# Recurrent branch of a hybrid decoder layer: v's rows turned a step later, scan first in the next step, a norm's end behind the splits, sample sums a step later

## The chip, the cores and the metric

The kernel runs on one core of one Trainium2 chip. The metric is the device time of one execution in microseconds (us), as the median of several runs; a profiled execution stands beside it. Engines are named as the profile does: PE (TensorE matmul), PEld (its weight load), DVE (VectorE), ACT (ScalarE), POOL (GpSimd), SP (SyncE, which issues most DMAs).

## The reference, cut to what matters

One decoder layer is computed for 512 prompt tokens and 8 sample tokens together (520 columns): a dilated window attention and a recurrent branch side by side, a gated merge, and a mixture of experts. The recurrent branch has 8 heads with keys and values of 128:

```
q_hg = silu(qh);  f = lb + (1 - lb) * sigmoid(fh);  k_hg = 1 - f;  logf = log(f)
b = cumsum(logf)                                     # per chunk
attn[t,s] = sum_k q[t] k[s] exp(b[t] - b[s])         # s <= t
o = (q * exp(b)) @ state + attn @ v
new_state = exp(b_last) * state + (k * exp(b_last - b))^T v
hg = rms_norm(o, hg_norm_w) * silu(gh)               # per head
y = sigmoid(ga) * (att @ w_br_a) + sigmoid(gb) * (hg @ w_br_b)
```

The samples take one step each from their own cached state (`hgrn_s`); the attention's sample tokens read the three caches.

## The kernel before, in words

Everything lies transposed: channels on partitions, 520 columns along the free axis. Every product of the layer is made from two-part weights: a raw block of 128x1024 is loaded, ACT makes the high part (`whi`, L132), DVE the rest (`wlo`, L133), and PE runs 24 pairs of matmuls of 260 columns (`proj`, L180). `weights_in` keeps the loads four and the splits three blocks ahead, issuing them at the start of the step.

In the recurrent stage the order of every engine's queue is the order in which the program issues instructions. A head has five steps, each with one product: f, q, v, gg (the gate gh) and one block of the merge's gates (`gate`). Ahead of each product, `step_all` runs `beside`: first the DMAs left over by `after` in the step before, then the next piece of each running generator. The generators are `chain(h)`, one per head; each lives for ten steps, so two of them run at any time. `decode_attention` is a further generator, advanced once per step and twice in every fourth (SP loads cache rows, POOL multiplies, DVE sums).

The pieces of `chain(h)`, by the step in which they run: (q) logarithm on ACT, scan on DVE; (v) kd, exponentials, decays of levels 0 and 1; (gg) v's rows: one small transpose for the samples (`pts`, L783) and four for the prompt (`ptm`, L788), copied by ACT to `vs` and `vt`, then q times k (L800), sides 0 and 1, decays 2; (gate) k's rows `kt`, pair matmuls of levels 0 and 1 (L758, L761), decays 3, and the load of the sample states `ss`; (next f) pairs 2, decays 4 and 5; (q) pairs 3, sides 4 and 5, ACT scales `ss`; (v) pairs 4 and 5, `neighbours` (L746), and the sample sums, eight additions of v times k to `ss` on DVE (L836); (gg) pairs 6, the states (L846 on PE, L853 on DVE); (gate) the outputs `po` and `pos`, copied by ACT to `ob`, and its square; (f after that) `finish`: the norm's matmul (L383), the root on ACT (L384), reciprocal (L385), weighting (L386) and gate (L876) on DVE. `decays(i)` are two DVE subtractions (L733, L734) and an exponential on ACT (L735); `sides(i)` are two DVE products (L739, L740).

The matmuls of the chain write to four rotating banks (`bank`), the products to two double ones (`pair_bank`). The program outside this stage (from the splits of `att` and `hg` on) is ordered by the framework's own planner.

Of the kernel before, what the change touches and what calls it, by code (L numbers as in the profile page):

```python
# [11 lines left out]
F32 = mybir.dt.float32  # L12
# [5 lines left out]
AF = mybir.ActivationFunctionType  # L18
ALU = mybir.AluOpType
# [4 lines left out]
P = 128  # L24
D = 1024
KC = D // P
NT = 512
NS = 8
# [57 lines left out]
def layer(ctx, tc, A, O, K):  # L86
    nc = tc.nc
    act, dve, pool, pe, dma, dma2 = nc.scalar, nc.vector, nc.gpsimd, nc.tensor, nc.sync, nc.sync
# [4 lines left out]
    ident = cp.tile([P, P], F32, name="ident")  # L93
# [22 lines left out]
    d_hv = dr.tile([8, NS, P], F32, name="d_hv")  # L116
# [11 lines left out]
    def split(hi, lo, src, eng=None, first=None):  # L128
        if first:
            first.tensor_copy(hi, src)  # L130
        else:
            act.activation(hi, src, AF.Copy)  # L132
        return (eng or dve).tensor_tensor(out=lo, in0=src, in1=hi.bitcast(F32), op=ALU.subtract)  # L133
# [12 lines left out]
    def bank(name="pa"):  # L146
        return banks[-1].tile([P, 512], F32, tag="pa", name=name)
# [25 lines left out]
    def proj(src, kc, xhi, xlo, eng=None, w=None):  # L173
        whi, wlo = w or wload(src, kc, P, eng)
        ps = pair_bank()
        for k in range(kc):
            first, last = k == 0, k == kc - 1
            for w, x, n in ((whi, xhi, 0), (whi, xlo, 1), (wlo, xhi, 2)):
                for s in range(2):
                    pe.matmul(ps[:, s, :NH], w[:, k, :], x[:, k, s * NH:(s + 1) * NH],  # L180
                              start=first and n == 0, stop=last and n == 2)
        return ps
# [57 lines left out]
    hT_hi = fp.tile([P, KC, N], F32R, name="hT_hi")  # L240
    hT_lo = fp.tile([P, KC, N], F32R, name="hT_lo")


    with tc.tile_pool(name="st", bufs=1) as st:
# [9 lines left out]
        rs = st.tile([P, N], F32, name="rs")  # L254
# [31 lines left out]
    att = xp.tile([P, 4, N], F32, name="att")  # L286
# [53 lines left out]
    def weights_in():  # L340

        k = at_[2]
        at_[2] += 1
        while at_[0] < min(len(plan), k + 4):
            src, kc = plan[at_[0]]
            parts[at_[0]] = wtile("raw", F32, RAW)
            dma.dma_start(parts[at_[0]].rearrange("p (k c) -> p k c", k=kc), src)
            at_[0] += 1
        while at_[1] < min(len(plan), k + 3):
            hi, lo = wtile("whi", F32R, 3), wtile("wlo", F32R, 3)  # L350
            split(hi, lo, parts[at_[1]])
            parts[at_[1]] = [x.rearrange("p (k c) -> p k c", k=plan[at_[1]][1]) for x in (hi, lo)]
            at_[1] += 1
        return parts.pop(k)

    def product():
        return proj(None, KC, hT_hi, hT_lo, None, weights_in())

    late = []

    def after(f):

        late.append(f)

    def begin():
        todo, late[:] = late[:], []
        for f in todo:
            f()

    def norm_bc(x, lhsT, w, pl):  # L370

        sq = pl("sq", F32)
        act.activation(sq, x, AF.Square)
        parts = [sq]
        if lhsT.dtype == F32R:
            parts = pl("shi", F32R), pl("slo", F32R)
            split(*parts, sq, pool)

        def finish():
            ps, rs = pair_bank(), pl("rs", F32)  # L380
            for s in range(2):
                for i, t in enumerate(parts):
                    pe.matmul(ps[:, s, :NH], lhsT, t[:, s * NH:(s + 1) * NH], start=i == 0, stop=i == len(parts) - 1)  # L383
            act.activation(two(rs), half(ps), AF.Sqrt, bias=eps)  # L384
            dve.reciprocal(rs, rs)  # L385
            dve.scalar_tensor_tensor(out=x, in0=x, scalar=w, in1=rs, op0=ALU.mult, op1=ALU.mult)  # L386

        return finish

# [64 lines left out]
    with tc.tile_pool(name="at", bufs=2) as at:  # L454
# [9 lines left out]
        xs_, vtm, norms_ = {}, {}, {}  # L464
# [97 lines left out]
        def second_norms(hp):  # L562

            yield
            yield
            for n in range(6):
                norms_.pop((hp, n))()
                yield

        def qkv(hp, n):  # L570
# [116 lines left out]
    hg = mix.enter_context(tc.tile_pool(name="hgo", bufs=1, side="right")).tile([P, KC, N], F32, name="hg")  # L687
    with tc.tile_pool(name="da", bufs=2) as da, tc.tile_pool(name="hgp", bufs=2) as hp_:
# [10 lines left out]
        def t2(name):  # L699
            return hp_.tile([P, N], F32, tag="t2", name=name, bufs=T2)[:, :NT]  # L700

        w = hp_.tile([P, 9 * 64], F32, name="w", bufs=1)
# [6 lines left out]
        def chain(h):  # L709
            d = heads[h]  # L710
            f, k = d["f"], d["k"]
            lf = t2("lf")
            act.activation(lf, f[:, :NT], AF.Ln)
            bb = t2("bb")
            dve.tensor_tensor_scan(bb, reset, lf, 0.0, op0=ALU.mult, op1=ALU.add)
            yield
            q = d["q"]
            kd, eb = t2("kd"), t2("eb")
            bl = t128(bb)[:, :, P - 1:P]
# [59 lines left out]
            yield  # L779

            v = d["v"]
            pts = bank("pts")
            pe.transpose(out=pts[:NS, :P], in_=v[:, NT:], identity=ident)  # L783

            def rows(src, name):
                pt = bank("ptm")
                for i in range(4):
                    pe.transpose(out=pt[:, i * P:(i + 1) * P], in_=src[:, i * P:(i + 1) * P], identity=ident)  # L788
                dst = t2(name)
                act.activation(dst, pt, AF.Copy)  # L790
                return dst

            vs = hp_.tile([NS, P], F32, tag="vs", name="vs")
            act.activation(vs, pts[:NS, :P], AF.Copy)
            after(lambda: dma2.dma_start(d_hv[h], vs))
            vt = rows(v, "vt")
            pl = bank("pl")
            for a in range(4):
                c = slice(a * P, (a + 1) * P)
# [6 lines left out]
            sides(1)  # L806
            dve.tensor_mul(qb, q[:, :NT], eb)
            yield
            kt = rows(kd, "kt")
            placed = [pairs(0), pairs(1)]  # L810
            sides(2)
            decays(3)
            for x in placed:
                x()
            ss = hp_.tile([P, NS, P], F32, tag="ss", name="ss", bufs=2)
            dma2.dma_start(ss, A["state_hgrn"][h])
            vb = hp_.tile([P, NS, P], F32, tag="vb", name="vb", bufs=1)
            after(lambda: dma2.dma_start(vb, d_hv[h:h + 1].to_broadcast([P, NS, P])))
            yield
            placed = [pairs(2)]  # L820
            sides(3)
            decays(4)
# [9 lines left out]
            yield  # L832
            placed = [pairs(4), pairs(5)]
            neighbours()
            for b in range(NS):
                dve.scalar_tensor_tensor(out=ss[:, b], in0=vb[:, b], scalar=k[:, NT + b:NT + b + 1], in1=ss[:, b],  # L836
                                         op0=ALU.mult, op1=ALU.add)
            for x in placed:
                x()
            after(lambda: dma2.dma_start(O["hgrn_s"][h], ss))  # L840
            yield
            placed = pairs(6)
            pk = bank("pkv")
            for a in range(4):
                c = slice(a * P, (a + 1) * P)
# [3 lines left out]
            for a in range(4):  # L849
                c = slice(a * P, (a + 1) * P)  # L850
                new = hp_.tile([P, P], F32, tag="state", name="state", bufs=4)
                if a:
                    dve.scalar_tensor_tensor(out=new, in0=states[-1], scalar=eb[:, (a + 1) * P - 1:(a + 1) * P], in1=pk[:, c],  # L853
                                             op0=ALU.mult, op1=ALU.add)
                else:
                    dve.tensor_copy(new, pk[:, c])
                states.append(new)
            after(lambda: dma2.dma_start(O["hgrn_p"][h], states[3]))
            yield
            po = bank("po")  # L860
            for a in range(4):
                c = slice(a * P, (a + 1) * P)
# [7 lines left out]
            ob = hp_.tile([P, N], F32, tag="t2", name="ob", bufs=T2)  # L870
            act.activation(ob[:, :NT], po, AF.Copy, scale=0.5)
            act.activation(ob[:, NT:], pos[:, :NS], AF.Copy, scale=0.5)
            finish = norm_bc(ob, ones_v, half_w, lambda n, dt: hp_.tile([P, N], dt, tag="t2", name=n, bufs=T2))
            yield
            finish()
            dve.tensor_mul(hg[:, h], ob, d["gg"])  # L876

        decode = decode_attention(da)
        late_steps = [0]

        def step_all():
            beside()
            late_steps[0] += 1
            for _ in range(2 if late_steps[0] % 4 == 0 else 1):
                next(decode, None)


# [8 lines left out]
                    flows.append(chain(h + 1))  # L896
        while flows:
            step_all()
        begin()
        for _ in decode:  # L900
            pass
# [7 lines left out]
    a_hi = xp2.tile([P, 4, N], F32R, name="a_hi")  # L909
    a_lo = xp2.tile([P, 4, N], F32R, name="a_lo")  # L910
# [2 lines left out]
    y_hi = yp.tile([P, KC, N], F32R, name="y_hi")  # L913
    y_lo = yp.tile([P, KC, N], F32R, name="y_lo")
    for c in range(4):
        split(a_hi[:, c], a_lo[:, c], att[:, c], pool if c % 2 else dve)
    for c in range(KC):
        split(g_hi[:, c], g_lo[:, c], hg[:, c], pool if c % 2 else dve)
    for c in range(KC):
# [40 lines left out]
    for c in range(KC):  # L960
# [3 lines left out]
        if c == 0:  # L964
            with tc.issue_after(last.ins):
# [4 lines left out]
                                 op0=ALU.mult, op1=ALU.add)  # L970
# [11 lines left out]
    rs = yblk("rs")  # L982
# [334 lines left out]
    for k, _ in enumerate(choose_tile(3, sel3)):  # L1317
        if k % 3 == 0:
            ahead(pool)
    dve.scalar_tensor_tensor(out=idx3, in0=sel3[:, 1].rearrange("p h k -> p (h k)"), scalar=128.0,  # L1320
                             in1=sel3[:, 2].rearrange("p h k -> p (h k)"), op0=ALU.mult, op1=ALU.add)
# [91 lines left out]
    cs, vr, vs, gts = {}, {}, {}, {}  # L1413
# [61 lines left out]
    rows = [(k < P) + (20 <= k < 148) + (148 <= k < 156) + (160 <= k) for k in range(n_sparse)]  # L1475
# [44 lines left out]
    x = x_rows(d_x[3], P)  # L1520
# [71 lines left out]
```

## Time and profile before

| what | value |
|---|---|
| median of 3 runs | 2453.06 us (2452.21 to 2458.89) |
| profiled execution | 2453.66 us |
| its span | 2451.9 us |
| mean granted TensorE clock | 0.962 |
| PE busy | 2297.9 us (94%) |
| PEld busy | 2118.4 us (86%) |
| DVE busy | 1760.3 us (72%) |
| ACT busy | 1155.0 us (47%) |
| POOL busy | 660.6 us (27%) |

The span is the time from the first to the last instruction; the profiled execution's own time lies 1.8 us above it. Busy shares are means over the whole kernel, whose stages have different limits. A granted clock of 1.00 is 2.4 GHz, 0.50 is 1.2 GHz, and a value between is a mean over a stretch that held both.

### The profile page before, as it was taken

The page shows a single profiled execution, that of the slowest core. Times are in us where ns is not written, and L with a number is a line of the kernel's source. Part 1 is how long each engine was busy: PE and PEld are TensorE (multiplying, and loading weights), DVE is VectorE, ACT ScalarE, POOL GpSimd, SP SyncE. Part 2 cuts the span into 40 slices and gives each one's busy share as a digit, 9 for nine tenths or more (in the row PEclk, how much of TensorE's full clock was granted, in tenths as well). Part 3 has the DMA queues.
Part 4 walks back from the last instruction along what each step waited for, and adds up shares of the span by engine and source line. Part 5 has one row for each costly group of instructions (what it writes and reads, how often), then busy time and mean ns, then how long its engine had stood idle before and what let it go on. Part 6 is the DMA issues. An engine that isn't in the chain of part 4 may idle for free.

```text
span 2451.9 us, 37852 instructions
## 1 busy us (share of the span) xinstructions
PE 2297.9 (94%) x14547; PEld 2118.4 (86%) x14547; DVE 1760.3 (72%) x3156; ACT 1155.0 (47%) x1850; POOL 660.6 (27%) x450
## 2 busy tenths in 40 slices
PE   6899999999888988999978989999999999999997
PEld 3788999989888888989978989988888888888886
DVE  3677566548766665547998897477888878788876
ACT  3556566445444443243337778633333333333332
POOL 1110121102221223004450001034444445454433
PEclk9998999999899999999998999989999999999999
DMA  6453212234442324423344555779999999999996
GB/s 220 155 167 113 81 55 70 64 121 141 138 140 90 115 97 157 157 94 96 96 135 168 195 209 199 265 275 331 343 351 328 365 323 344 345 348 331 347 309 206
DMA packets 197466, 495.49 MB, mean 202 GB/s; under 512 B 18123, under 2 KB 84651, under 8 KB 195749
## 3 DMA queue, kind: packets, MB, share of 16 engines
q1 hardware_dynamic: 147636, 313.02, 38.0%
q0 software_dynamic: 39456, 143.28, 16.3%
q10 hardware_dynamic: 10192, 36.77, 4.0%
q8 instruction: 114, 1.87, 0.3%
q14 instruction: 68, 0.55, 0.1%
HBM read 439.17 MB, written 54.49 MB: 201 GB/s over the span
## 4 chain that ended last, share of the span: by engine, by line
PE 43%; DVE 7%; ACT 3%; DMA 1%; issue 1%; ACTq 0%; POOL 0%; POOLq 0%; DVEq 0%; SPq 0%
PE acc L1471 21%; PE ph L1091 16%; PE pp L180 3%; PE pp L1356 2%; ACT oa L1348 1%; DVE wlo L133 1%; ACT whi L132 1%; DVE e L1151 1%; ACT stage L1363 1%; DVE y L1121 1%; DVE sel L1153 0%; PE pt L1177 0%; DMA vr<-in_peer_v 0%; DVE oa L1342 0%; DVE e L1148 0%
## 5 line engine op out<-in xcount | busy, mean ns | idle before, releaser
L133 DVE TENSOR_TENSOR wlo<-raw,whi 128x1024 fp32r<-128x1024 f32 (+1 forms) x254 | 320.0, 1265 | 176.4 <-ACT whi L132 175.2
L1245 POOL DMA_INDIRECT gat<-in_peer_u,idx x128 | 212.6, 1661 | 628.1 <-DVE junk L1272 442.2
L1091 PE MATMUL ph<-h_hi,whi 128*128 128x384 f32 x1024 | 356.4, 348 | 13.4 <-ACT whi L132 13.4
L1091 PE MATMUL ph<-h_hi,wlo 128*128 128x384 f32 x1024 | 351.8, 344 | 8.4 <-POOL wlo L133 7.3
L1091 PE MATMUL ph<-h_lo,whi 128*128 128x384 f32 x1024 | 350.7, 342 | 0.0
L132 ACT ACTIVATE whi<-raw 128x1024 fp32r<-128x1024 f32 (+1 forms) x284 | 292.8, 1036 | 111.3 <-PE pp L180 58.9
L180 PE MATMUL pp<-hT_hi,whi 128*128 128x260 f32 x1344 | 287.9, 297 | 17.2 <-ACT whi L132 17.1
L180 PE MATMUL pp<-hT_hi,wlo 128*128 128x260 f32 x1344 | 280.0, 291 | 5.1 <-DVE wlo L133 5.1
L180 PE MATMUL pp<-hT_lo,whi 128*128 128x260 f32 x1344 | 279.7, 291 | 0.0
L180 PEld LDWEIGHTS pp<-hT_hi,whi 128*128 128x128 f32 x1344 | 218.7, 199 | 20.3 <-ACT whi L132 18.6
L180 PEld LDWEIGHTS pp<-hT_hi,wlo 128*128 128x128 f32 x1344 | 216.6, 197 | 6.9 <-DVE wlo L133 6.9
L180 PEld LDWEIGHTS pp<-hT_lo,whi 128*128 128x128 f32 x1344 | 217.5, 198 | 0.0
L1091 PEld LDWEIGHTS ph<-h_hi,whi 128*128 128x128 f32 x1024 | 197.4, 193 | 17.8 <-ACT whi L132 14.9
L1091 PEld LDWEIGHTS ph<-h_hi,wlo 128*128 128x128 f32 x1024 | 197.0, 192 | 10.4 <-POOL wlo L133 7.9
L1091 PEld LDWEIGHTS ph<-h_lo,whi 128*128 128x128 f32 x1024 | 197.1, 192 | 2.8
L1471 PE MATMUL acc<-vhi,chi 128*128 128x512 f32 x768 | 195.8, 390 | 0.0
L1471 PE MATMUL acc<-vhi,clo 128*128 128x512 f32 x768 | 195.0, 389 | 0.0
L1471 PE MATMUL acc<-vlo,chi 128*128 128x512 f32 x768 | 194.9, 389 | 0.0
L133 DVE TENSOR_TENSOR vlo<-vr,vhi 128x1024 fp32r<-128x1024 f32 x128 | 156.3, 1221 | 52.7 <-ACT vhi L132 52.7
L132 ACT ACTIVATE vhi<-vr 128x1024 fp32r<-128x1024 f32 x128 | 135.3, 1057 | 114.6 <-PE acc L1471 114.6
L1095 ACT ACTIVATE ge<-ph 128x384 f32<-128x384 f32 x128 | 62.6, 489 | 264.9 <-PE ph L1091 264.5
L1245 POOL DMA_INDIRECT gat<-in_peer_v,idx x128 | 162.7, 1271 | 70.9 <-issue 34.0
(378 smaller groups left out, 4531.9 us busy)
## 6 DMA issues: line engine op xcount, KB each, us to landing
raw<-in_uT SPq DMA_DIRECT2D x128, 512.0 KB
vr<-in_peer_v SPq DMA_DIRECT2D x128, 512.0 KB
raw<-in_w_in SPq DMA_DIRECT2D x84, 512.0 KB
raw<-in_w_ada SPq DMA_DIRECT2D x48, 512.0 KB
d_G<-stage ACTq DMA_DIRECT2D x12, 2048.0 KB
gt<-d_G SPq DMA_DIRECT2D x32, 768.0 KB
d_ge<-ge ACTq DMA_DIRECT2D x56, 192.0 KB
ge<-d_ge SPq DMA_DIRECT2D x56, 192.0 KB
```

The source lines that it names most:

```text
L132: act.activation(hi, src, AF.Copy)
L133: return (eng or dve).tensor_tensor(out=lo, in0=src, in1=hi.bitcast(F32), op=ALU.subtract)
L180: pe.matmul(ps[:, s, :NH], w[:, k, :], x[:, k, s * NH:(s + 1) * NH], start=first and n == 0, stop=last and n == 2)
L1091: pe.matmul(ph[:, :NB], w[:, k], x[:, k, :NB], start=k == 0 and n == 0, stop=k == KC - 1 and n == 2)
L1095: act.activation(ge, ph[:, :NB], AF.Gelu_apprx_tanh)
L1121: dve.match_replace(out=y[:n], in_to_replace=vals[:, 0:8], in_values=x, imm_value=-3.0e38)
L1151: dve.tensor_tensor(out=e3[:n], in0=e3[:n], in1=pb[:n, :, None, :].to_broadcast([n, H, 16, 16]), op=ALU.mult)
L1245: pool.indirect_dma_start(out=t, out_offset=None, in_=A[tab][0], in_offset=bass.IndirectOffsetOnAxis(ap=idx, axis=0))
L1348: act.activation(oas[g][:, j], oas[g][:, j], AF.Copy, scale=sels[t][:, 0, n + j:n + j + 1])
L1356: pe.matmul(pgs[g // 2][:, g % 2, j * P:(j + 1) * P], oa[:, j], ob[:, j], start=True, stop=True)
L1363: act.activation(st[:, :, n0:n0 + 8], pgs.pop(b).rearrange("p s (n i) -> p i (s n)", i=P), AF.Copy)
L1471: pe.matmul(acc[2 * t + d], a[:, t * P:(t + 1) * P], b[:, d * 512:(d + 1) * 512], start=first and n == 0, stop=last and n == 2)
```

## The change

Five things move; no instruction's arithmetic changes.

- The transposes of v (`pts` and `vt`), the copies and the write of `d_hv` go from the gg piece to the gate piece, ahead of the pair matmuls; k's rows go behind them. The read of `vb` goes one piece later as well.
- The scan goes from the end of the first piece to the start of the second.
- The sample sums go from the v piece to the gg piece, behind the states; the write of the sample states goes with them.
- `finish` now issues the norm's matmul and the root, and returns the rest (reciprocal, weighting, gate). That rest is kept in `ends` and issued by `product` behind `weights_in`, so behind the splits of the step.
- The decode is advanced twice in every third step, and the low parts of `att` (`a_lo`) are all made on DVE, where two of four were on POOL.

```
+    ends = []
+
+    def end():
+        while ends:
+            ends.pop(0)()
+
     def product():
-        return proj(None, KC, hT_hi, hT_lo, None, weights_in())
+        w = weights_in()
+        end()
+        return proj(None, KC, hT_hi, hT_lo, None, w)
...
             act.activation(two(rs), half(ps), AF.Sqrt, bias=eps)
-            dve.reciprocal(rs, rs)
-            dve.scalar_tensor_tensor(out=x, in0=x, scalar=w, in1=rs, op0=ALU.mult, op1=ALU.mult)
+
+            def rest():
+                dve.reciprocal(rs, rs)
+                dve.scalar_tensor_tensor(out=x, in0=x, scalar=w, in1=rs, op0=ALU.mult, op1=ALU.mult)
+
+            return rest
...
-                norms_.pop((hp, n))()
+                norms_.pop((hp, n))()()
...
             bb = t2("bb")
+            yield
             dve.tensor_tensor_scan(bb, reset, lf, 0.0, op0=ALU.mult, op1=ALU.add)
-            yield
...
-            pts = bank("pts")
-            pe.transpose(out=pts[:NS, :P], in_=v[:, NT:], identity=ident)
...
-            vs = hp_.tile([NS, P], F32, tag="vs", name="vs")
-            act.activation(vs, pts[:NS, :P], AF.Copy)
-            after(lambda: dma2.dma_start(d_hv[h], vs))
-            vt = rows(v, "vt")
...
             yield
-            kt = rows(kd, "kt")
+            pts = bank("pts")
+            pe.transpose(out=pts[:NS, :P], in_=v[:, NT:], identity=ident)
+            vs = hp_.tile([NS, P], F32, tag="vs", name="vs")
+            act.activation(vs, pts[:NS, :P], AF.Copy)
+            after(lambda: dma2.dma_start(d_hv[h], vs))
+            vt = rows(v, "vt")
             placed = [pairs(0), pairs(1)]
             sides(2)
             decays(3)
             for x in placed:
                 x()
+            kt = rows(kd, "kt")
             ss = hp_.tile([P, NS, P], F32, tag="ss", name="ss", bufs=2)
             dma2.dma_start(ss, A["state_hgrn"][h])
+            yield
             vb = hp_.tile([P, NS, P], F32, tag="vb", name="vb", bufs=1)
             after(lambda: dma2.dma_start(vb, d_hv[h:h + 1].to_broadcast([P, NS, P])))
-            yield
...
             neighbours()
-            for b in range(NS):
-                dve.scalar_tensor_tensor(out=ss[:, b], in0=vb[:, b], scalar=k[:, NT + b:NT + b + 1], in1=ss[:, b],
-                                         op0=ALU.mult, op1=ALU.add)
             for x in placed:
                 x()
-            after(lambda: dma2.dma_start(O["hgrn_s"][h], ss))
...
                 states.append(new)
+            for b in range(NS):
+                dve.scalar_tensor_tensor(out=ss[:, b], in0=vb[:, b], scalar=k[:, NT + b:NT + b + 1], in1=ss[:, b],
+                                         op0=ALU.mult, op1=ALU.add)
+            after(lambda: dma2.dma_start(O["hgrn_s"][h], ss))
...
-            finish()
-            dve.tensor_mul(hg[:, h], ob, d["gg"])
+            rest = finish()
+
+            def gated():
+                rest()
+                dve.tensor_mul(hg[:, h], ob, d["gg"])
+
+            ends.append(gated)
...
-            for _ in range(2 if late_steps[0] % 4 == 0 else 1):
+            for _ in range(2 if late_steps[0] % 3 == 0 else 1):
...
             step_all()
+            end()
...
-        split(a_hi[:, c], a_lo[:, c], att[:, c], pool if c % 2 else dve)
+        split(a_hi[:, c], a_lo[:, c], att[:, c], dve)
```

## Rows read from the trace of the kernel before

**Rows 1.** Windows, 530 to 960 us: length, busy time of each engine, clock

```profile
core 0: us, PE busy (x) PEld busy (x) DVE busy (x) ACT busy (x) POOL busy (x), PEclk, DMA share, GB/s
530.00:960.00 430.00, 375.27 (x2912) 367.30 (x2910) 288.17 (x517) 212.08 (x332) 93.76 (x67) 0.91 0.40 132
```

**Rows 2.** Waits, 530 to 962 us: who waited for whom; total, times, longest

```profile
DVE rs L385 <- ACT rs L384: 44.4, 8, 8.1
...
DVE bb L715 <- ACT lf L713: 28.8, 7, 4.8
...
PE pts L783 <- ACT v L434: 26.4, 7, 5.4
...
PE pl L761 <- DVE w L740: 7.4, 8, 1.9
...
PE pl L761 <- DVE w L746: 3.6, 3, 2.7
...
ACT whi L132 <- DMA raw<-in_w_in: 1.8, 1, 1.8
...
PE pkv L846 <- DVE am L773: 0.5, 1, 0.5
```

**Rows 3.** Timeline of ACT, 643 to 668 us: start, length, instruction, idle before

```profile
643.95 1.30 ACT L735 ACTIVATE w<-w 128x512 f32<-128x512 f32 x2 [5.04 <-DVE w L734]
...
656.19 0.61 ACT L441 ACTIVATE q<-pp 128x520 f32<-128x520 f32 x1
664.22 0.63 ACT L721 ACTIVATE kd<-kd 128x512 f32<-128x512 f32 x1 [7.42 <-DVE kd L720]
...
667.26 0.58 ACT L434 ACTIVATE v<-pp 128x520 f32<-128x520 f32 x1
```

**Rows 4.** Timeline of DVE, 653 to 664 us

```profile
653.96 1.22 DVE L715 TENSOR_TENSOR_SCAN bb<-reset,lf 128x512 f32<-128x512 bf16 x1 [4.31 <-ACT lf L713]
...
660.31 2.17 DVE L836 SCALAR_TENSOR_TENSOR ss<-vb,k,ss 128x128 f32<-128x128 f32 x8
```

**Rows 5.** Timeline of PE, in two products, pairs of matmuls

```profile
649.58 0.40 PE L180 MATMUL pp<-hT_lo,whi 128*128 128x260 f32 x2
649.82 0.40 PE L180 MATMUL pp<-hT_hi,wlo 128*128 128x260 f32 x2
...
671.07 0.64 PE L180 MATMUL pp<-hT_lo,whi 128*128 128x260 f32 x2
671.50 0.64 PE L180 MATMUL pp<-hT_hi,wlo 128*128 128x260 f32 x2
```

**Rows 6.** Windows with a low clock: length, PE busy, clock, DMA share, GB/s

```profile
612.00:620.00 8.00, 5.91 (x31) 0.57 0.48 131
660.00:674.00 14.00, 9.89 (x46) 0.51 0.50 164
718.00:725.00 7.00, 5.05 (x24) 0.51 0.39 111
776.00:780.00 4.00, 4.00 (x22) 0.57 0.08 26
830.00:835.00 5.00, 4.28 (x24) 0.66 0.13 46
888.00:893.00 5.00, 5.00 (x30) 0.66 0.14 29
789.00:794.00 5.00, 5.00 (x30) 0.66 0.01 3
```

**Rows 7.** Timelines of DVE and PE at the stage's end

```profile
952.90 3.40 DVE L385 RECIPROCAL rs<-rs 128x520 f32<-128x520 f32 x1 [1.80 <-ACT rs L384]
...
957.13 0.70 DVE L876 TENSOR_TENSOR hg<-ob,gg 128x520 f32<-128x520 f32 x1
...
959.28 0.80 PE L180 MATMUL pp<-a_hi,whi 128*128 128x260 f32 x2 [7.68 <-ACT a_hi L132]
```

**Rows 8.** Waits of SP's queue, 530 to 962 us

```profile
SPq L840 <- DVE am L773: 96.8, 8, 24.8
```

**Rows 9.** The tile bb: durations in ns, least, median, most

```profile
L733 DVE TENSOR_TENSOR w<-bb x48: 402/417/1483, 538.0 to 917.6; 128x256 f32<-128x256 f32 x48
```

## The prediction

> **What bounds the kernel now.** I read the page first, then the chain of waits, the windows of one stretch, and the timelines of its engines. Over the whole span PE is the busiest engine, but the change touches only the recurrent branch, so I looked for that stretch: it runs from about 530 to 960 us. There PE works 375.3 of 430 us, DVE 288.2, ACT 212.1, and the mean granted clock is 0.91 [rows 1]. No engine other than PE is near full, so what can be won are the 55 us in which PE stands still and the time in which it runs at the lower clock.
>
> The list of waits says for whom PE stands still [rows 2]: 26.4 us in seven waits before the transposes of v (L783), for ACT's copy of v; 7.4 us before the pair matmuls (L761) for the products of L740; 3.6 us before the last pair matmul for DVE's L746; 0.5 us before L846. The same list shows the cause further back: DVE stands 44.4 us for the root of the norm (L384) and 28.8 us for the logarithm (L713). Since each engine works through its queue in order, whatever stands behind such a wait is late. One head shows it. ACT waits 5.04 us at 643.95 for DVE's decays, then works without a break to 656.80 (twelve groups, the first and the last shown); then it waits 7.42 us for kd, and only at 667.26 does it copy v [rows 3]. DVE began the scan at 653.96 after 4.31 us for the logarithm, with split, q's product, neighbours and sample sums (2.17 us) behind it, and kd behind those [rows 4]. So v's rows wait for the whole chain.
>
> The clock adds to it. At the upper level, 2.4 GHz, the starts of two pairs of matmuls lie 0.24 us apart; at the lower, 1.2 GHz, 0.43 us [rows 5]. A microsecond of product at the lower clock thus costs 1 - 0.24/0.43 = 0.44 us. Six windows around a wait at L783 show clocks from 0.51 to 0.66 [rows 6] (the first six rows): twice the missing clock times the length gives 6.9, 13.7, 6.9, 3.4, 3.4 and 3.4 us, together 37.7. PE stood still for 2.1 + 4.1 + 1.9 + 0.7 = 8.8 of them, so it worked 28.9 us slowly and lost 12.7.
>
> **The change part by part.** *v's rows.* The five transposes, their two copies and the write of d_hv go one step later. The work is the same, so it costs nothing by itself; what goes is the wait, -26.4 us. After the product of v, PE still has its own last pair matmul, the key sums, q times k and another product, so v has more than a step to be copied; nothing of the 26.4 remains in that place.
>
> *Scan first in the next step, sample sums a step later.* DVE no longer stands at the scan with q's product and the neighbours behind it, and eight sums (2.17 us) leave the queue ahead of kd [rows 4]. The waits for L746 and at L846 go: -4.1 us. The sums now stand ahead of the next sides and decays, so ACT's exponential there is 2.2 us later; the cover is PE's product of that step, and without it that would be 2.2 us per head.
>
> *Norm's end behind the splits.* Reciprocal, weighting and gate take 957.83 - 952.90 = 4.9 us of DVE [rows 7]. They stood ahead of the sides and decays of the next head, which explains both ACT's 5.04 us and six of the eight waits for L740, at 0.8 us each: -4.9 of the 7.4. What is late next is the pair matmul two steps on, for now the 4.9 us stand ahead of *its* sides. ACT's unbroken run begins some 5 us earlier, so q and kd come that much earlier too.
>
> *Clock.* With the waits at L783 gone I give back the 12.7 us behind six of them. The falls without a long wait stay: one window of 5 us at 0.66 shows PE busy throughout, right after the many short matmuls of a gate step [rows 6] (the last row).
>
> The Trainium skill ("TensorE: Matmul & The Clock Gate", section "Part 1: The HAM clock gate") says that the clock is throttled by default and released by sustained work. The falls after waits agree with it; in the window without a wait the record of busy time does not decide, so I go by the row. By the page alone no new falls would come, and the sum below would be 3.0 us better.
>
> *DMAs.* Three on SP move: the write of d_hv, the read of vb and the write of the sample states, one of each per head. Distance between write and read stays one step. The wait at the head of SP's queue for L840, 96.8 us with 24.8 the longest, is there now as well [rows 8], and behind it wait weights, taps and queries; yet ACT waited only 1.8 us for weights in all [rows 2]. I take 0; if that cover goes in every head, 7 x 1.8 = 12.6.
>
> *Decode two steps every third time, and a_lo on DVE.* The decode issues the same instructions, finished some steps earlier; its column sums then no longer stand behind the last norm. At the end PE starts at 959.28, 1.45 us behind the last gate's end at 957.83 [rows 7]. a_lo still comes on DVE behind that gate, so I take -1.5 and no more; the bounds are 0 and the whole 7.7.
>
> Removed: 26.4 + 4.1 + 4.9 + 12.7 + 1.5 = 49.6 us.
>
> *New waits.* PE now arrives earlier everywhere, and DVE has to follow. The trace does not show these places. Two look tight: the pair matmuls behind the norm's end, and the gate step, where the short matmuls now take seven banks out of four (two for the outputs, two for v's rows, two for the pairs, one for k's rows) and so wait for ACT's copies of the first ones. The bounds are 0 and 26.4/7 = 3.8 us per head, the wait removed. DVE's own jitter is the nearest row: the same decay takes 0.42 us in the median and 1.48 at most [rows 9]. I take one such lengthening, 1.1 us per head, seven times: +7.7.
>
> *New falls.* The gate step gets a longer run of short matmuls. I allow two more falls of 3.4 us: 2 x 3.4 x 0.44 = +3.0. The bounds are 0 and seven as long as the longest (9.6 us of work): 29.6.
>
> Sum: -49.6 + 7.7 + 3.0 = -38.9. The profiled execution took 2453.66 us, 0.6 above the median of the runs, so the forecast is 2414.8.
>
> **The rivals.**
> *Full cover.* No new wait and no fall. At clock 0.91 the stretch held 0.18 x 430 = 77 us of the lower clock; less the 37.7 already counted, 39.7 more would give 17.5. With it -49.6 - 17.5 = -67, or 2387. For it: ACT and DVE have room. Against it: the fall without a wait. A mild form, no new waits but the old falls, gives 2404.
>
> *The wait only moves.* Each head keeps 3.8 us in the gate step or at the pair matmuls, and seven falls of 3.4 us come with it: -49.6 + 26.4 + 10.5 = -12.7, or 2441. For it: DVE's lengthened operations, and sums now ahead of the sides.
>
> *The change does not do what it says.* The loop through ACT and DVE sets the head's length, not PE's wait; v's wait is then replaced in full, clock included: 2453 within 7. Against it: two waits of DVE, 44.4 and 28.8, are work that the new order puts elsewhere.
>
> *Slower.* The gate step: a pair matmul there needs a bank that ACT must empty, behind an exponential that now waits for the sample sums. The 49.6 are used up at 7.1 us per head. A wait of 5.4, the longest at L783, plus the longest fall (9.6 x 0.44 = 4.2) makes 9.6 per head: +67.2 - 49.6 = +17.6, or 2471. Against it: the copies are short and the product before the gate step covers them.
>
> **How the numbers follow.** A change of 0.3%, about what a measurement of this kernel can tell from none, is 7.4 us. The likeliest case, 2400 to 2430, gets 0.62, full cover 0.10, a wait that moves 0.17, no effect 0.06, slower 0.05. All but the last two are faster by more than 7.4 us: 0.89; same 0.06; slower 0.05. The range takes in the moved wait above and, below, full cover but for 3 us: 2390 to 2441; left out are no effect, slower and part of full cover, together under 0.2.
>
> **What would show it.** In the profile after: no wait before L783 for v; DVE's waits for the root and the logarithm down by more than half; ACT's copy of v before the pair matmuls of the next step end; PE's idle time in the stretch near 27 us (55 less 35.4, plus 7.7) and its mean clock at 0.94; the stretch some 37 us shorter and all that follows unchanged. It is wrong if PE waits in the gate step for ACT's copies or before L761 for DVE, by more than 2 us per head, or if the clock falls once per head all the same.

## The result and the profile after

| | before | after |
|---|---|---|
| median of 4 runs each | 2452.64 us (2451.18 to 2458.89) | 2416.51 us (2415.32 to 2419.38) |
| profiled execution, its span | 2453.66, 2451.9 us | 2419.38, 2417.6 us |
| mean granted clock | 0.962 | 0.965 |

The ratio is 0.9846 with a 95% interval of 0.9831 to 0.9861: the change takes off 36 us, and the forecast of 2414.8 lies 2 us from the median.

The page of the changed kernel, its span and the busy time of its engines:

```profile
span 2417.6 us, 37836 instructions
PE 2285.3 (95%) x14547; PEld 2106.4 (87%) x14547; DVE 1762.8 (73%) x3158; ACT 1153.4 (48%) x1850; POOL 656.7 (27%) x448
```

The recurrent stage ends with the first product on `a_hi`. It started at 959.28 [rows 7]; the timeline of after around that point (start, duration, engine, operation, idle time before it):

```profile
923.22 0.70 DVE L891 TENSOR_TENSOR hg<-ob,gg 128x520 f32<-128x520 f32 x1
924.77 0.80 PE L180 MATMUL pp<-a_hi,whi 128*128 128x260 f32 x2 [7.87 <-ACT a_hi L132]
```

It now starts at 924.77, 34.5 us earlier. The span is 34.3 us shorter, so all of the gain lies in this stage, and what follows it is unchanged. The stage has no sharp start, and an execution reaches it some us sooner or later than another (525 to 534 us here). Where kernels are compared below, its length runs from the attention's last matmul of 128 columns (`po<-pt`, L545 in before; at 529.0 us there, at 528.4 in after) to the first product on `a_hi`: 430.3 us before, 396.4 after, 33.9 less. All kernels below run the same 2922 matmuls between these points, one of them with some added (in two, one record is missing). The stage and three stretches of it, by the windows of after:

```profile
core 0: us, PE busy (x) PEld busy (x) DVE busy (x) ACT busy (x) POOL busy (x), PEclk, DMA share, GB/s
530.00:925.00 395.00, 361.93 (x2905) 356.42 (x2905) 289.08 (x514) 208.50 (x330) 93.20 (x65) 0.93 0.44 144
577.00:582.00 5.00, 4.99 (x29) 4.99 (x30) 4.09 (x9) 2.06 (x3) 1.29 (x1) 0.66 0.00 0
707.00:718.00 11.00, 4.88 (x24) 4.89 (x25) 8.33 (x21) 1.57 (x2) 0.00 (x0) 0.53 0.42 149
751.00:756.00 5.00, 5.00 (x31) 5.00 (x31) 4.86 (x7) 0.00 (x0) 2.20 (x2) 0.66 0.00 0
```

PE's idle time is 395 - 361.9 = 33.1 us where before (530 to 959.28) had 429.3 - 374.6 = 54.7. For the clock I went through the stage in windows of one microsecond and added up PE's busy time, each times the share of the lower level (twice the missing clock): 40.1 us of work at the lower clock, against 58.6 before. At the prediction's 0.44 us for each this is 8.1 us.

The waits of after in the stage (engine, line waited for; us in total, times, longest), with DVE's wait for the root last:

```profile
PE pc L653 <- DVE sc L647: 9.1, 1, 9.1
PE pp L180 <- ACT a_hi L132: 7.9, 1, 7.9
PE pl L770 <- ACT w L747: 5.6, 1, 5.6
PE pl L773 <- DVE w L752: 5.4, 5, 1.5
PE ptm L798 <- DVE am L785: 1.8, 1, 1.8
PE ptm L798 <- ACT vs L818: 1.3, 1, 1.3
PE pl L773 <- ACT whi L132: 0.9, 1, 0.9
PE ptm L798 <- DVE am L811: 0.8, 1, 0.8
PE pl L770 <- ACT ob L883: 0.3, 1, 0.3
...
DVE rs L395 <- ACT rs L392: 1.8, 1, 1.8
```

Beside [rows 2] the reader is to see three things. The wait for v's copy (26.4) and the one for L746 are gone. DVE's wait for the root is 1.8 instead of 44.4, and the one for the logarithm does not appear any more. And one wait is new in this size: 9.1 us for a product of the decode (`pc`, a transpose of the scores' sums `sc`).

One head, ACT and then DVE (timelines of after; ACT's before are [rows 3], DVE's [rows 4]):

```profile
687.01 0.60 ACT L448 ACTIVATE f<-pp 128x520 f32<-128x520 f32 x1 [0.21 <-PE pp L180]
...
700.26 0.63 ACT L733 ACTIVATE kd<-kd 128x512 f32<-128x512 f32 x1 [3.99 <-DVE kd L732]
...
703.31 0.58 ACT L446 ACTIVATE v<-pp 128x520 f32<-128x520 f32 x1
```

```profile
686.67 3.39 DVE L395 RECIPROCAL rs<-rs 128x520 f32<-128x520 f32 x1
690.10 0.76 DVE L396 SCALAR_TENSOR_TENSOR ob<-ob,half_w,rs 128x520 f32<-128x520 f32 x1
690.90 0.70 DVE L891 TENSOR_TENSOR hg<-ob,gg 128x520 f32<-128x520 f32 x1
691.52 0.42 DVE L751 TENSOR_TENSOR w<-w,q 128x256 f32<-128x256 f32 x1
...
698.32 1.19 DVE L728 TENSOR_TENSOR_SCAN bb<-reset,lf 128x512 f32<-128x512 bf16 x1
...
706.48 2.18 DVE L867 SCALAR_TENSOR_TENSOR ss<-vb,k,ss 128x128 f32<-128x128 f32 x8
...
712.39 0.67 DVE L647 TENSOR_REDUCE sc<-pr 67x8 f32<-67x512 f32 x1
```

The reciprocal and the scan show no idle time ahead of them: root and logarithm were ready when DVE came. ACT still waits 3.99 us for kd (7.42 before). The eight sample sums now stand among the work ahead of `sc` at 712.39; that is the one for which PE waits 9.12 us at 713.12, in the middle of the window 707 to 718 whose clock is 0.53.

### The profile page after: what moved, and what is told of

Same layout as the page of the kernel before. It is cut to its first block, busy times and chain, and to the rows that moved or that the text cites. A ratio compares the mean times of both kernels' runs of the same rounds, so it can differ in the third digit from the quotient of the medians.

```text
span 2417.6 us, 37836 instructions
## 1 busy us (share of the span) xinstructions
PE 2285.3 (95%) x14547; PEld 2106.4 (87%) x14547; DVE 1762.8 (73%) x3158; ACT 1153.4 (48%) x1850; POOL 656.7 (27%) x448
## 4 chain that ended last, share of the span: by engine, by line
PE 43%; DVE 7%; ACT 3%; DMA 1%; issue 1%; ACTq 0%; POOL 0%; POOLq 0%; DVEq 0%; SPq 0%
PE acc L1489 21%; PE ph L1109 17%; PE pp L180 3%; PE pp L1374 2%; ACT oa L1366 1%; DVE wlo L133 1%; ACT whi L132 1%; DVE e L1169 1%; ACT stage L1381 1%; DVE y L1139 1%; DVE sel L1171 0%; DMA vr<-in_peer_v 0%; PE pt L1195 0%; DVE e L1166 0%; DVE oa L1360 0%
## 5 line engine op out<-in xcount | busy, mean ns | idle before, releaser
L1109 PEld LDWEIGHTS ph<-h_hi,wlo 128*128 128x128 f32 x1024 | 197.1, 192 | 10.2 <-POOL wlo L133 7.7
```

What stands on the lines that cost most here:

```text
L1109: pe.matmul(ph[:, :NB], w[:, k], x[:, k, :NB], start=k == 0 and n == 0, stop=k == KC - 1 and n == 2)
```

## The experiments

Two theories stood against each other. By the first, the prediction's own (theory A below), each wait has its own cause, so that the parts add up: v's rows are worth 26.4 us and their clock, the norm's end 4.9, scan and sums 4.1. By its rival (theory B) the waits are one chain: the norm's end on DVE holds up the next head's sides and decays, these hold up ACT, which is late with the logarithm, kd and v's copy; whichever part frees the chain first takes the gain of the others. A third question was the clock: do the falls go with the waits?

All kernels side by side: the ratio and its interval from the runs; then, from one profiled execution each and in us, the stage's length between the two points named above, PE's idle time in it, and "slow", its work at the lower clock (no idle time is given where added matmuls fill it):

| kernel | ratio to before | 95% | length | idle | slow |
|---|---|---|---|---|---|
| before | 1 | | 430.3 | 54.7 | 58.6 |
| after | 0.9846 | 0.9831 to 0.9861 | 396.4 | 33.1 | 40.1 |
| v's rows alone | 0.9899 | 0.9884 to 0.9914 | 406.8 | 36.1 | 50.0 |
| norm's end alone | 0.9835 | 0.9818 to 0.9852 | 390.8 | 27.7 | 38.6 |
| scan and sums alone | 0.9956 | 0.9942 to 0.9970 | 421.1 | 48.3 | 53.7 |
| before, waits filled | 0.9975 | 0.9963 to 0.9987 | 422.5 | | 35.3 |
| after without v's rows | 0.9859 | 0.9842 to 0.9877 | 390.5 | 32.9 | 24.4 |
| after without norm's end | 0.9947 | 0.9932 to 0.9962 | 418.0 | 45.1 | 54.0 |
| after, decode as before | 0.9835 | 0.9820 to 0.9850 | 393.8 | 28.5 | 42.8 |
| after, `pc` a step later | 0.9835 | 0.9818 to 0.9853 | 388.8 | 25.7 | 41.1 |
| after less two, a product held back | 0.9798 | 0.9785 to 0.9811 | 381.6 | 20.9 | 31.2 |
| norm's end, a product held back | 0.9806 | 0.9793 to 0.9819 | 386.9 | 24.9 | 35.0 |
| norm's end, reciprocal twice | 0.9945 | 0.9933 to 0.9957 | 416.1 | 42.9 | 56.7 |
| norm's end behind the sides | 0.9826 | 0.9814 to 0.9839 | 388.2 | 29.2 | 29.4 |

**Each part alone on the kernel before.** First v's rows, k's rows behind the pairs, and `vb` a piece later:

```
-            pts = bank("pts")
-            pe.transpose(out=pts[:NS, :P], in_=v[:, NT:], identity=ident)
...
-            vt = rows(v, "vt")
...
-            kt = rows(kd, "kt")
+            pts = bank("pts")
+            pe.transpose(out=pts[:NS, :P], in_=v[:, NT:], identity=ident)
...
+            vt = rows(v, "vt")
             placed = [pairs(0), pairs(1)]
...
+            kt = rows(kd, "kt")
```

> The kernel before with one part alone: v's rows (and with them d_hv, vb and the place of k's rows) a step later. Theory A, each part takes its own wait: the 26.4 us before L783 and the 12.7 us of lower clock behind them go, 2413 to 2426 us, and the other waits of PE for DVE (L740, L746, some 11 us) stay as they are. Theory B, the parts share one chain (norm's end, decays, q, kd, v) and PE only meets it at the next place: 5 to 15 us gained, 2438 to 2448, and the waits of PE at the pair matmuls or at k's rows grow to over 20 us.

Then the norm's end alone:

```
+        w = weights_in()
+        end()
+        return proj(None, KC, hT_hi, hT_lo, None, w)
...
-            finish()
-            dve.tensor_mul(hg[:, h], ob, d["gg"])
+            rest = finish()
...
+            ends.append(gated)
```

> The kernel before with one part alone: the norm's end behind the splits. Theory A: six waits of 0.8 us at L761 go and nothing else, about 5 us, 2448. Theory B: the norm's end heads the chain that makes v late, so ACT comes some 5 us per head earlier and most of the 26.4 us before L783 go without v's rows being moved: 25 to 38 us, 2415 to 2428, with under 8 us left before L783.

And the scan and the sample sums:

```
-            dve.tensor_tensor_scan(bb, reset, lf, 0.0, op0=ALU.mult, op1=ALU.add)
             yield
+            dve.tensor_tensor_scan(bb, reset, lf, 0.0, op0=ALU.mult, op1=ALU.add)
...
             neighbours()
-            for b in range(NS):
...
                 states.append(new)
+            for b in range(NS):
```

> The kernel before with the scan first in the next step and the sample sums a step later, nothing else. Theory A: the waits for L746 and at L846 go, about 4 us, 2448. Theory B: the sums (2.2 us) leave DVE's queue ahead of kd, so v is 2 us per head earlier, about 15 us, 2438, with some 12 us left before L783.

Measured: 0.9899, 0.9835, 0.9956. The norm's end alone gives what the whole change gives (0.9846; the intervals overlap); the three together would make 25 + 40 + 11 = 76 us if they added up, and the change makes 36. Not every expectation came true: v's rows alone, at 2433 us, lie between the ranges of the two theories; the norm's end alone has the time of theory B, but 12.4 us left at v where it allowed 8; the scan and the sums, at 2446, lie near theory A. The waits of the kernel with v's rows alone:

```profile
PE pl L761 <- DVE w L740: 7.2, 9, 1.4
...
PE pl L761 <- DVE w L746: 3.6, 3, 2.7
...
DVE rs L385 <- ACT rs L384: 34.8, 8, 7.7
...
DVE bb L715 <- ACT lf L713: 23.6, 7, 4.8
```

PE no longer waits for v, but DVE still stands 34.8 us for the root and 23.6 for the logarithm. With the norm's end alone:

```profile
PE pts L795 <- ACT v L446: 12.4, 5, 4.5
...
PE pl L773 <- DVE w L752: 1.0, 1, 1.0
...
DVE bb L727 <- ACT lf L725: 7.4, 2, 3.7
```

v's rows stand where they stood, and still PE's wait for v fell from 26.4 to 12.4, the products of L740 (L752 here) cost 1.0 instead of 7.4, and DVE's wait for the logarithm went from 28.8 to 7.4. ACT's wait for DVE's decays (L734, L746 here) is 38.9 in all where the kernel before had 69.2. One move thus shortened waits in four places. With scan and sums alone PE's wait for v is 21.1 and DVE's for the root 42.6, where before has 26.4 and 44.4.

**One part taken out of the change.** v's rows put back to the gg piece:

```
+            pts = bank("pts")
+            pe.transpose(out=pts[:NS, :P], in_=v[:, NT:], identity=ident)
...
+            vt = rows(v, "vt")
...
-            pts = bank("pts")
-            pe.transpose(out=pts[:NS, :P], in_=v[:, NT:], identity=ident)
...
-            vt = rows(v, "vt")
+            kt = rows(kd, "kt")
             placed = [pairs(0), pairs(1)]
...
-            kt = rows(kd, "kt")
```

> The changed kernel with v's rows back in their old step; everything else changed. Theory A (each part takes its own wait, so 26 to 39 us hang on v's rows): 0.990 to 1.000 of the time before, 2432 to 2457 us where before stands at 2456. Theory B (one chain, which the norm's end heads, so that the move of v's rows is spare once that is out of the way): 0.980 to 0.986, as fast as the changed kernel or faster, with under 8 us left before the small transpose of v.

And the norm's end straight behind the root:

```
-            ends.append(gated)
+            gated()
```

> The changed kernel with the reciprocal, the weighting and the gate straight behind the root, as before; everything else changed. Theory A: only the six waits of 0.8 us at the pair matmuls come back, 5 us, 0.987. Theory B: DVE stands for the root again with the next head's sides and decays behind it, and what is left is what v's rows bring without it, 0.989 to 0.992 (rows alone: 0.990), with DVE's wait for the root back above 30 us.

Measured: 0.9859 without v's rows, not to be told from the whole change (0.9846); 0.9947 without the norm's end, 25 us slower than the whole and slower than either theory expected. PE's wait for v comes back with 5.8 us in four places when the rows go back, and the rest of the kernel is no worse for it. The waits without the norm's end:

```profile
ACT w L747 <- DVE w L746: 100.0, 22, 9.2
...
DVE rs L395 <- ACT rs L392: 33.0, 8, 6.2
...
PE pl L773 <- DVE w L752: 13.0, 12, 2.1
PE pc L653 <- DVE sc L647: 12.2, 3, 10.0
```

ACT stands 100.0 us for DVE's decays (67.0 in after), and PE's waits for L752 are twelve where [rows 2] had eight. This kernel is 12 us slower than v's rows alone, although it has the scan and the sums moved as well. The prediction had a price for such a case, the sums ahead of the sides and no cover. But PE's waits at the pair matmuls, 13.4 us with those for the neighbours, are only 2.6 more than the 10.8 with v's rows alone. What grew is the wait of the decode's transposes `pc`, from 3.7 to 12.2 us, nearly all of the 9.0 us by which PE's idle time differs. So the decode, advanced more often here, is the likelier cause: in the changed kernel the old cadence takes this wait from 9.1 to 2.8 us (below). The kernel without the norm's end and with the old cadence was not tried.

**Where the norm's end holds the chain.** In the kernel with the norm's end alone, it was put behind the sides and decays, but ahead of the split:

```
             beside()
+            end()
             late_steps[0] += 1
```

> The kernel before with the norm's end behind the other head's sides and decays, but ahead of the split of the step. If it is the sides and decays (and so ACT's exponentials, f and q) that the norm's end held up, this is as good as behind the splits, 0.982 to 0.986. If it is the split and the product that wait for it, most of the gain is lost, 0.992 or above.

0.9826, the same as behind the split (0.9835). So it is the sides and decays that the norm's end held up, and the split need not be ahead of it.

Then a second reciprocal was set in front of the true one; its result is not used:

```
             def rest():
+                if lhsT.dtype != F32R:
+                    dve.reciprocal(hp_.tile([P, N], F32, tag="again", name="again", bufs=1), rs)
                 dve.reciprocal(rs, rs)
```

> The kernel before with the norm's end behind the splits and a second reciprocal of 3.4 us (its result unused) ahead of the true one, eight times in this stage. Theory B says that place and not load mattered: behind the splits DVE has room, so 0 to 8 us more than the norm's end alone, 0.9835 to 0.987. If DVE's load sets the length of a head, all 27 us show, 0.994 or above.

0.9945, 25 to 27 us more than without it, by the medians and by the ratios: 3.2 to 3.4 per head, about as much as the added reciprocal takes. So the second expectation came true, against theory B: not only the place of the norm's end counts but also DVE's load, and there is no room behind the splits. The timelines of this kernel, DVE first:

```profile
791.79 3.39 DVE L396 RECIPROCAL again<-rs 128x520 f32<-128x520 f32 x1
795.22 3.40 DVE L397 RECIPROCAL rs<-rs 128x520 f32<-128x520 f32 x1
...
800.61 0.42 DVE L754 TENSOR_TENSOR w<-w,k 128x256 f32<-128x256 f32 x1
...
801.18 1.97 PE L775 MATMUL pl<-w 128*128 128x64 f32 x16 [1.80 <-DVE w L754]
```

PE waits 1.80 us in the pair matmuls for the sides behind the norm's end, in six heads 12.5 in all: the wait that the prediction placed there. PE's idle time grew by 15.2 and its slow work by 18.1, at 0.44 another 8.0: together 23 of the 25.3 us by which the stage is longer.

**The clock by itself.** In the kernel before, 14 matmuls of 512 columns were put ahead of the sample transpose of seven heads; their results are overwritten by it. PE works there instead of waiting; v comes no earlier:

```
             pts = bank("pts")
+            for _ in range(14 if h else 0):
+                pe.matmul(pts, hT_hi[:, 0, :P], hT_hi[:, 0, :512], start=True, stop=True)
```

> The kernel before with 14 added matmuls of 512 columns (results overwritten, output unchanged) in PE's queue where it waits for v, in seven heads. They last about 3 us, less than six of the seven waits, so no wait is removed and the order of the other engines stays. If the lower clock behind those waits is worth 12.7 us and comes from PE standing still, the time falls to about 2440 and the clock stays at 1.00 behind the waits. If the clock falls for another reason, or costs nothing because PE waits later anyway, the time stays at 2452 to 2456.

0.9975, 6 us less (3 to 9) and between the two expectations, where the prediction's clock term behind these waits was 12.7. Two of the places by the windows (columns: start to end, length, PE busy, clock, DMA share, GB/s):

```profile
core 0: us, PE busy (x), PEclk, DMA share, GB/s
612.00:620.00 8.00, 6.45 (x50) 1.00 0.43 117
660.00:674.00 14.00, 13.52 (x87) 0.88 0.52 161
```

The first is whole where [rows 6] show a fall around the wait; in the second some of the fall stays, at the start of the filling. So the falls there do follow from the standing PE. The 6 us understate what that is worth, for the filling has a cost of its own: in the first head it lasts 3.4 us where PE had waited 0.6, and the transposes start at 562.20 with v ready at 559.79, 2.4 us late. With these the clock gave back some 8.5 us (5 to 11), and in the profiled execution 10.2, since the stage is 7.8 us shorter there. The term was thus too large by 2 to 4 us, and the interval reaches from less than half of it to nearly the whole. Over the stage 35.3 us of slow work remain, nearly all in places without such a wait.

**The new wait of the decode.** The decode advanced twice in every fourth step again:

```
-            for _ in range(2 if late_steps[0] % 3 == 0 else 1):
+            for _ in range(2 if late_steps[0] % 4 == 0 else 1):
```

> The changed kernel with the old cadence of the decode (twice in every fourth step). In the changed kernel PE waited 9.1 us in one place for the sum of the decode (L653 for L647), which now falls in a step where eight other DVE groups stand ahead of it, and 4.5 us of work behind it ran at the lower clock. If the cadence put it there, this kernel loses that wait and runs some 11 us shorter, 0.980. If the wait comes from the new order of DVE's queue whatever the step, it stays above 5 us and the time stays at 0.984 to 0.986.

And, instead, the transpose of the scores' sums one step later:

```
         vt = taps(0, 0, 1)
+        yield
         pc = bank("pc")
```

> The changed kernel with the decode's transposes (L653) one turn of the decode later than the last sum that they read. Whatever put the wait there, the sum is then a step old: the 9.1 us and the lower clock behind them go, 0.980 (11 us less than the changed kernel). If PE only meets the same lateness of DVE at its next wait, 0.984 to 0.986.

`pc` costs 2.8 in two waits in the one, 4.7 (for another tile) in the other. Both measure 0.9835, 2.7 us better than the change, within its interval and between the two expectations. In the profiled executions more of it arrives: PE's idle time fell by 4.6 and 7.4 us, and the stage is 2.6 and 7.6 us shorter. But the second of them reached the stage 5.4 us later than after did, by work that the edit does not touch, and ends no sooner. A gain of a few us is of the size of such differences, and these runs cannot say how much of the 9.1 us came off the time.

**A better version.** Without v's rows, with the decode as before, and with the last gate product of the stage held back behind the last head's chain, to stand where PE waits for `a_hi`:

```
-            ... [partial(gate, i) for i in GT[h]]):
+            ... [partial(gate, i) for i in (GT[h] if h < 7 else GT[h][:-1])]):
...
             step_all()
+            if not flows:
+                gate(GT[7][-1])
             end()
```

> The changed kernel with v's rows in their old step, the old cadence of the decode, and the last gate product of the last head held back by one step, so that PE has work while the last norm's end runs. The waits for the decode's sum (7 to 9 us) and most of the 7.9 us before the branch products go, with the lower clock behind them: 0.977 to 0.980 of the time before, faster than every kernel so far. If PE only stands elsewhere (before the norm's matmul, which then has no product ahead of it), 0.983 to 0.986.

0.9798, or 2408.3 us, the fastest of all. Its timeline at the end of the stage:

```profile
909.62 0.40 PE L180 MATMUL pp<-hT_hi,wlo 128*128 128x260 f32 x2
...
912.94 0.51 PE L180 MATMUL pp<-a_hi,whi 128*128 128x260 f32 x2 [2.14 <-ACT a_hi L132]
```

PE waits 2.14 us there instead of 7.87, because the held product runs to 910 while DVE ends the last norm. The same product held back in the kernel with the norm's end alone:

> The kernel before with the norm's end behind the splits (0.9835 alone) and the last gate product held back by one step, nothing else. If the last product fills the wait at the end, 5 to 8 us less than with the norm's end alone, 0.980 to 0.982; if not, 0.983 to 0.985. Against e9 it tells what scan, sums and a_lo on DVE still bring: by theory B under 5 us.

0.9806 against 0.9835: 7 us, though the two intervals just touch; the wait for `a_hi` fell from 7.7 to 2.1. The two best kernels cannot be told apart. So two edits, the norm's end and the held product, give 48 us, and v's rows, the scan, the sums and the decode are not needed for it.

## Why the prediction was right, and where it was not

The total came out, though not term by term:

| term | predicted | measured |
|---|---|---|
| wait for v (L783) | -26.4 | -26.4 |
| L746 and L846 | -4.1 | -4.1 |
| L740 (L752 after) | -4.9 | 7.4 to 5.4: -2.0 |
| clock, falls removed and new | -12.7 + 3.0 | 18.5 us less slow work, at 0.44: -8.1 |
| stage end | -1.5 | PE's wait for `a_hi` 7.7 to 7.9: +0.2 |
| new waits | +7.7 | +10.9 |
| sum | -38.9 | -29.5 of 33.9 |

The new waits are `pc` (9.1, where three such waits had 3.3 in all), the gate step (1.8, 0.8 and 0.3), one of 1.3 for `vs` and one of 0.9 for a weight split. At the stage's end PE starts 0.85 us behind the last gate, 0.6 sooner than before, but stands as long as it did. The wait of 5.6 before the first transposes of k's rows, which the prediction did not count, is there after as well, in front of the first pairs. Between the sum of the records and the gain of the stage 4.4 us are left: PE's busy time fell by 375.6 - 363.3 = 12.3 us for the same 2922 matmuls, and the clock at 0.44 explains 8.1 of it. The 0.44 is too low. Over the thirteen kernels that run these matmuls and no others, PE's busy time (length less idle in the table) grows by 0.54 us with each us of slow work (a straight line through them, off by at most 2.1 us), which makes it 10.0. So some of the nearness of the total is luck. By its terms the sum is 9.4 us short, all of them but the two removed waits on the same side; 4.4 of that came back in PE's work, 1.9 of it because slow work costs more than reckoned, and the new waits, not far from their 7.7, arose for the most part in the decode, for which the prediction had no term.

What it said of the profile: no wait at L783, right. Root and logarithm down by more than half, right (44.4 to 1.8, 28.8 to none). Idle time near 27, measured 33.1, high by `pc`. Clock 0.94, measured 0.93. The stage 37 us shorter, measured 33.9, all after it unchanged. ACT's copy of v before the end of the next step's pair matmuls, wrong: it ends at 703.89, and these pairs, started at 700.94, end at 701.9; nobody waits for it. Of the two tight places, the gate step costs 2.9 in all and the pair matmuls behind the norm's end 5.4, both far under 2 us per head. The sign that the clock might fall once per head all the same came nearer: by the windows of one microsecond there are eight separate falls with PE at work in the eight heads, where before has twelve. The new wait of any size was at a place that the prediction had not looked at, the decode.

The step that failed is the credit of the parts. The prediction put 26.4 us and the clock behind it on *v's rows*, and 4.9 on *the norm's end behind the splits*. Alone, the norm's end is worth 40 us and v's rows 25; in the company of the rest v's rows are worth nothing that can be measured (0.9859 without, 0.9846 with) and the norm's end 25. The prediction read the right sentence off the trace, that whatever stands behind DVE's wait for the root is late, and wrote down only the 4.9 us of DVE's work behind the root; the 44.4 us of DVE waiting in front of the reciprocal, with sides and decays in the queue behind it, were not charged to that part (behind the splits 1.8 of them are left). They came out through ACT as late logarithms, late kd and a late v. The total was right all the same, because each wait that the change removes was counted once, whichever edit removes it.

"The loop through ACT and DVE sets the head's length", the ground of the rival of no effect, was the better account of the mechanism; its price was wrong, since the norm's end is itself one of the changes and opens that loop. The doubled reciprocal shows how near it lies: 3.4 us more on DVE per head cost 3.2 to 3.4 us per head.

Not settled: how much of the time the decode's wait is worth; why the kernel without the norm's end is slower than v's rows alone; and why ACT starts `a_hi` only behind the last gate's `hg`. In the program the pool of `a_hi` is opened only once the pool of the recurrent branch is closed, but whether that holds it was not tried.

## What to carry to other kernels

Sum the waits that an order removes once, over the whole chain of queues, and do not divide them among the edits: the edits stand in for each other, and only a run of each alone and one with each left out tells which is needed. Where an engine waits for another in the middle of its queue, the cost of that place is the wait with everything queued behind it, not the work that follows; put the work that others wait for ahead of it. At the end of a stage, hold one independent product back to cover the last serial piece.

## What the runs showed of the hardware

The granted clock does not fall once per wait. In after it is 0.66 from 577 to 582 and from 751 to 756 with PE recorded busy in all but 0.01 us of ten, and PE's work at the lower clock was anything from 24.4 to 58.6 us in kernels that run the same matmuls in the stage. Over the thirteen of them each us of it went with 0.54 us more of PE's busy time. Filling seven waits with matmuls took away nearly all of the falls behind six of them, which had cost 12.7 us by the windows; 6 us came out as time, beside 2.4 that the filling itself cost, and falls remained elsewhere. How much slow work a kernel has is what one profile tells least: after and after without v's rows cannot be told apart in time (0.9846 and 0.9859), and have 40.1 and 24.4 us of it.
